# Head jobs as block products: eight of twelve instead of four of twelve, with sums formed in place

## The chip, the cores and the metric

The kernel runs on one core of one Trainium2 chip. A core has five engines that work side by side, each in its own order, and wait for one another through semaphores: TensorE (PE) does the matrix products (its loads of the stationary operand are listed apart, as PEld), VectorE (DVE), ScalarE (ACT) and GpSimd (POOL) do elementwise work, SyncE (SP) issues most of the transfers. The metric is the time of one execution of the whole program on the device, in microseconds (us); lower is better.

## What is computed

The reference is one layer of a hybrid decoder step in float32, for a prompt of 1024 tokens and 32 sample tokens (8 sequences of 4), with a width of 1024:

```python
h, gate = adaln_in(x, c, w_ada, b_ada, g_norm)         # RMS norm with scale and shift from c
(mq, mk, mv, mi, mf, mo, mz, aq, ak, av, az, gm, ga) = split_in(h @ w_in)
y_m, C, n, m = mlstm_branch(mq, mk, mv, mi, mf, mo, mz, ...)   # 4 heads, chunks of 128
q = partial_rope(aq, pos); k = partial_rope(ak, pos)
o = attn_prompt(q, k, v, sinks)                        # window of 128, 8 heads on 2 kv heads
y_a = o * silu(az)
u = sigmoid(gm) * (y_m @ w_mo) + sigmoid(ga) * (y_a @ w_ao)
x = x + gate * (u @ w_o)                               # then a final RMS norm
```

The sample tokens go through the same layer with a state (`state_C`, `state_n`, `state_m`) and a key and value cache of their own. Each operand of a large product is split into a high and a low half of reduced width; a product is the sum of three: high by high, high by low, low by high.

## The kernel before, in words

Tokens lie along the free dimension: 1024 prompt tokens and 32 sample tokens are 1056 columns, the channels lie on the 128 partitions in 8 tiles (k-tiles). The first stage normalises the input in 16 half tiles of 512 columns (`xT[token half][k]`), splits each into `h_hi` and `h_lo` (`y{p}_{k}` names the normalised tile) and also stores it to DRAM (`hD`). Every projection of h is then a *job* of 128 output channels.

A **plain job** (`job`, `piece`, L507 and L553) works through all 1056 columns in pieces of 384, 384 and 288: for each piece 8 k-tiles times three products, 72 matmuls. The jobs run in this order: `ak` and `av` with the first stage; the four query jobs `aq`; then of the twelve head jobs (`mq`, `mk`, `mv` for each of 4 heads) the first eight.

A **pair** (`Pair`, `block_products`, L1333 and L1483) takes two jobs together as a 2 x 2 block product, after the scheme of Winograd: two jobs by two halves of the contraction, times two contraction halves by two token halves, with seven products in place of eight. One product is 4 k-tiles times three, at 512 columns: 84 matmuls for a pair. It needs sums of weight blocks (formed per pair on VectorE) and the sums `t1` to `t4` of blocks of h, formed once by `sum_blocks` (L1292), which loads h from `hD` into tiles `hb`. The sample columns of a pair are 16 small products `smp` and a product `smpo` that adds them up. The products run in the order 1, 5, 6, 2, 7, 3, 4; `bx`, `bz`, `bw` and `by` are their accumulators, and `filled` copies one accumulator into the next as a start value. The 16 pairs before are: two `head_in` pairs (the last four head jobs), eight gate pairs (`ga` with `gm`), two query gate pairs (`az`), four head gate pairs (`mo` with `mz`). After them come the output products of attention (`ax` to `az`, from block sums that `att_sums` forms of the gated attention rows) and of the mLSTM branch (`g_w_mo`), then the last product (`fo`).

Between these main products stands the **side work**: 16 attention units (`unit`), four heads of the mLSTM prompt (`head`), the sample heads (`sample_head`), the conditioning of the gate (`ada_gate`), the output weights (`out_weights`), the block sums. Each is a generator. PE's order is the program's order (`mm` at L258, `tr` at L263), and a planner, `Side` (L112), decides while the program is written: it keeps a clock of estimated PE time, and after each k-tile `tick` lets due generators take a step. The streams "m" (heads and their gap), "a" (attention units: at most five at once), "x", "s" (sample heads, one at a time) and "g" each have their limits. `side.until` (L157) moves that clock forward and takes steps with no main product between them until a condition holds. The hook of the pairs (near L1966) uses it: product 6 of the last head gate pair is not written before all sample heads are done, since that pair's `samples` uses their results.

A sample head (L1152) ends with these steps: `st` (a PE product that sums its numerators), a copy to `sns` and its squared length on ScalarE, a dozen and a half small VectorE instructions (`fsden`, `fsv`, `fsr_y`, `fsr_w`), the scaling of `sns`, and the PE transpose `sty`. VectorE's, ScalarE's and POOL's order after the first stage is set by the framework's scheduler, as the instructions' operands come due; their instructions all carry L219. SP issues the transfers (L246) in its order, and some are issued on ACT's or POOL's queue.

Of the kernel before, what the change touches and what calls it, by code (L numbers as in the profile page):

```python
# [172 lines left out]
def body(tc, a):  # L173
    nc = tc.nc
    with ExitStack() as ctx:
        cp = ctx.enter_context(tc.tile_pool(name="cp", bufs=1))
        sp = ctx.enter_context(tc.tile_pool(name="sp", bufs=1))
# [13 lines left out]
            return ps.tile(shape, F32, tag="o", bufs=2, name=name)  # L191

        def ht(shape, name, dt=F32):
            return sp.tile(shape, dt, tag="half", bufs=43, name=name)

        def sm(shape, name, bufs=3, dt=F32):
            return sp.tile(shape, dt, tag=name, bufs=bufs, name=name)
# [43 lines left out]
        def dma(out, in_, late=False):  # L241
            stores(in_.tensor)
            issue(out, in_, late)

        def issue(out, in_, late=False, eng=None):
            ins = (eng or nc.sync).dma_start(out, in_)  # L246
            ins = getattr(ins, "ins", ins)
            if late:
                no_sync(ins, free)
                free.clear()  # L250
            free.append(ins)

        side = Side(stores, {"m": (2, 35.0), "a": (5,8.0), "x": (2, 0.0), "s": (1, 0.0), "g": (1, 0.0)}, 1.5)
# [47 lines left out]
        xT = [[], [], None]  # L301
# [183 lines left out]
        def raw_tile(name):  # L485
            return granule(name, "wr", 9)
# [61 lines left out]
        order = []  # L548
# [254 lines left out]
            dma(a["k_s"][124:128].rearrange("t b e -> b t e"), kns)  # L803
            dma(a["v_s"][124:128].rearrange("t b e -> b t e"), vns)

        heads_done, samples_done, units_done, products_done = [], [], [], []
        oD = [dp.tile([128, SEQ], F32, name=f"oD{g}") for g in range(4)]
        osm = cp.tile([128, NH, NS], F32, name="osm")
        yaD = [dp.tile([128, T], F32, name=f"yaD{g}") for g in range(4)]
# [176 lines left out]
        def head_jobs(h):  # L986
            q, k, v = mD[h]

            def keep(dst, smp, scale, eng):
                def ev(p, acc, c0, n):  # L990
                    t = ht([128, 384], f"mk{h}")[:, :n]
                    if eng == "v":
                        V.tensor_copy(t, acc[:, :n])
                    else:
                        S.activation(t, acc[:, :n], AF.Copy, scale=scale)
                    m = n if p < 2 else 256
                    issue(dst[:, c0:c0 + m], t[:, :m], eng=nc.scalar)
                    if p == 2:
                        G.tensor_copy(smp[:, h], t[:, 256:288])
                return ev  # L1000

            for n, dst, smp, scale in (("mq", q, qs, float(128 ** -0.5)), ("mk", k, ks, 1.0), ("mv", v, vs, 1.0)):
                if (n, h) not in order:
                    return
                i = order.index((n, h)) - order.index(None)
                if i == -4:
                    side.add("x", sum_blocks())
                if i == -1:
                    side.finish("g")
                    sc_bank[:] = po, "o+"  # L1010
                    next(work)
                job((n, h), keep(dst, smp, scale, "s"), (lambda: next(work)) if i == -1 else None)
                head_part(h, 2)
# [3 lines left out]
        def head_part(h, n):  # L1017
            parts_done[h] += n
            if parts_done[h] == 6:
                side.add("m", head(h))  # L1020
# [252 lines left out]
        blocks, formed = {}, []  # L1273
        def block(kh, th):
            return [tuple(x(4 * kh + k, 512 * th, 512) for x in (h_hi, h_lo)) for k in range(4)]

        def block_load(names, k):
            ts = []
            for kh, th in names:
                ts.append(ht([128, 512], f"hb{kh}{th}_{k}"))  # L1280
                dma(ts[-1], hD[:, 4 * kh + k, HALF[th]])
            return ts
# [6 lines left out]
        def block_tiles(n, k):  # L1289
            blocks[n].append(tuple(ht([128, 512], f"{n}{x}{k}", F32R) for x in "hl"))  # L1290

        def sum_blocks():  # L1292
            names = "t3", "t2", "t4"
            for n in names:
                blocks[n] = []
            load = lambda k: block_load(((0, 0), (0, 1), (1, 0), (1, 1)), k)
            nxt = load(0)
            yield 7.0, ""
            for k in range(4):
                b11, b12, b21, b22 = nxt  # L1300
                for n in names:
                    block_tiles(n, k)
                V.tensor_tensor(b22, b22, b12, op=ALU.subtract)
                yield 2.5, ""
                V.tensor_tensor(b11, b11, b22, op=ALU.add)
                V.tensor_tensor(b21, b21, b11, op=ALU.subtract)
                yield 5.0, ""
                if k < 3:
                    nxt = load(k + 1)
                for n, t in zip(names, (b22, b11, b21)):  # L1310
                    block_split(n, k, t)
                    yield 2.5, ""
            formed.append("t2")
            load = lambda k: block_load(((0, 0), (0, 1)), k)
            ts = [load(0), load(1)]
            yield 3.0, ""
            for b11, b12 in ts:
                V.tensor_tensor(b12, b12, b11, op=ALU.subtract)
            while not products_done:
                yield 0.5, ""  # L1320
            for k in range(4):
                b11, b12 = ts[k]
                if k > 1:
                    V.tensor_tensor(b12, b12, b11, op=ALU.subtract)
                block_split("t1", k, b12)
                if k < 2:
                    ts.append(load(k + 2))
                yield 1.5, ""
            formed.append("t1")
# [3 lines left out]
        class Pair:  # L1333
# [6 lines left out]
            def load(self):  # L1340
                for c, n in enumerate(self.names):
                    for kh in range(2):
                        t = self.raw[c, kh] = raw_tile(f"wr_{n[0]}{n[1]}_{kh}")
                        dma(t, a["w1"][JOBS[n]][:, 4 * kh:4 * kh + 4])
# [210 lines left out]

        order += [("ak", 0), ("av", 0)] + [("aq", g) for g in range(4)]
        inner = [(n, h) for h in range(NH) for n in ("mq", "mk", "mv")]
        paired = list(zip(inner[8::2], inner[9::2]))
        order += inner[:8]
        order += [None] + [("w_mo", d) for d in range(KT)]  # L1560


# [333 lines left out]
        def ada_gate():  # L1896
            s9 = cst[:, C_S9:C_S9 + 9]
            for j in range(2):
                cj = slice(j * 512, (j + 1) * 512)
                raws = []  # L1900
                for k in range(KT):
                    raws.append(ht([128, 512], f"adar_ga{j}{k}"))
                    dma(raws[-1], a["w_ada"][4 + j, :, k])
                    yield 2.0, ""
                gb = ht([128, 512], f"gb{j}")[:9]
                dma(gb, a["b_gate"][:, cj].to_broadcast((9, 512)))
                yield 5.0, "b"
                mS = ht([128, 512], f"adas_ga{j}")
                yield from ada_rows(raws, f"ga{j}", mS)
                yield 1.5, "b"  # L1910
                gp = pb([128, 512], f"gp{j}")[:9]
                mm(gp, s9, mS, start=True, stop=True)
                V.tensor_tensor(gb, gp, gb, op=ALU.add)
                V.tensor_scalar(gb, gb, 0.25, None, op0=ALU.mult)
                dma(gbD[:, cj], gb[0:1])
                for t in range(NT):
                    dma(gsD.rearrange("(b t) e -> b t e", t=NT)[:, t, cj], gb[1:9])
                yield 3.0, "b" if j == 0 else ""
            dma(c32, hD[:, :, SEQ:T])
# [46 lines left out]
        def hook(n, i):  # L1966
            if n == 0 and i in (6, 5):
                side.until(lambda: {6: "t2", 5: "t1"}[i] in formed)
            if i == 6:
                if pairs[n].kind is query_gate:  # L1970
                    side.until(lambda: len(units_done) == 16)
                side.until(lambda: len(samples_done) >= {head_in: 0, gate: 0, query_gate: 1, head_gate: pairs[n].i + 2}[pairs[n].kind])
            if (n, i) == (OUT_WEIGHTS, 6):
                side.add("g", out_weights())
# [2 lines left out]
            if n == len(pairs) - 1:  # L1977
                next(att, None)

        OUT_WEIGHTS = 4  # L1980
        LOADS = [(len(pairs) - 2, 7), (len(pairs) - 1, 5)]
        work = block_products(pairs, hook)
        att = att_products()
        for g in range(4):
            queries(g)
        side.add("g", ada_gate())
        side.add("s", sample_attention(), "b")
        blocks["t1"] = block(0, 1)
        for h in range(NH):
            head_jobs(h)  # L1990

# [62 lines left out]
        for d in range(KT):  # L2054
# [3 lines left out]
            for j in range(min(22, d * 26 // KT), min(22, (d + 1) * 26 // KT)):  # L2058
                n, k = parts[j]
# [104 lines left out]
        for i, r in enumerate(blocks_of_rows):  # L2164
            nxt = blocks_of_rows[i + 1] if i < 3 else None
# [64 lines left out]
            else:  # L2230
# [9 lines left out]
                for f, (y, (c0, n)) in enumerate(zip(Y, parts)):  # L2240
# [3 lines left out]
                    if f:  # L2244
                        V.tensor_tensor(xb[1][:, hi], xb[1][:, hi], gf[:, hi], op=ALU.mult)
                        half = norm_sum(ss[:, 2:4], 1, 2)
# [51 lines left out]


def build(d):  # L2300
    nc = bacc.Bacc("TRN2", target_bir_lowering=False, num_devices=1)
    aps = {}
    for k, v in d.items():
        aps[k] = nc.dram_tensor(k, v.shape, mybir.dt.from_np(v.dtype), kind="ExternalInput").ap()
    for k, s in OUTS.items():
        aps[k] = nc.dram_tensor(k, s, F32, kind="ExternalOutput").ap()
    with tile.TileContext(nc) as tc:
        body(tc, aps)
    return nc
# [19 lines left out]
```

## Time and profile before

| | before |
|---|---|
| median of three runs | 845.72 us (845.09 to 845.74) |
| span of the profiled execution (first to last instruction) | 843.1 us |
| PE busy | 823.9 us, 5185 instructions |
| DVE, ACT, POOL busy | 599.2, 416.0, 63.3 us |
| granted TensorE clock, mean of the span | 0.997 |
| first product of the first pair (`bx`) | 279.4 us |
| last `st` and last `sty` of a sample head | 621.1 and 634.2 us |

The three runs are times of the whole execution; of the profiled one the page gives the span alone, 2.6 us below the median of the runs. In a row of the time line stand the start in us, the duration, the engine, the line, the operation, the tile written and the tiles read with their shapes, the count of merged instructions, and, in brackets, how long the engine stood idle before and who released it. Matmuls overlap in PE, so a row's duration (0.39 for 512 columns) is longer than the distance to the next start.

### The profile page before, as it was taken

The numbers are of one execution on the slowest core, as the hardware profiler recorded it, in microseconds if no ns is written. First come the engines' busy times: TensorE is split into PE (matmuls) and PEld (weight loads), VectorE is DVE, ScalarE is ACT, GpSimd is POOL, SyncE is SP. The second block draws the span as 40 slices with busy tenths as digits, with TensorE's granted clock in tenths as the row PEclk, the third lists the DMA queues.
The fourth block names the chain that finished last, engine by engine and source line by source line (L and its number), as shares of the span: only waits on it lengthen the run. The fifth ranks groups of instructions, "written<-read, shape, count | busy, mean of one in ns | idle before, by whom it ended". The sixth has DMA issues, their size and how long they took to land.

```text
span 843.1 us, 15367 instructions
## 1 busy us (share of the span) xinstructions
PE 823.9 (98%) x5185; PEld 680.6 (81%) x5185; DVE 599.2 (71%) x1601; ACT 416.0 (49%) x1027; POOL 63.3 (8%) x108
## 2 busy tenths in 40 slices
PE   6999999999999999999999999999999999999996
PEld 3779999879989878888878777777777779997775
DVE  4887884556667586655766875788878998865676
ACT  5663346655655454554543534444436554334343
POOL 0120000000110000000000000000002104250000
PEclk9999999999999999999999999999999999999998
DMA  9996548337745653454656584556446586634522
GB/s 332 371 358 200 146 150 297 119 111 237 247 133 177 193 163 103 162 175 153 206 185 207 194 253 127 178 151 152 127 126 211 190 266 212 215 95 168 200 106 107
DMA packets 117859, 158.18 MB, mean 188 GB/s; under 512 B 29056, under 2 KB 64512, under 8 KB 117748
## 3 DMA queue, kind: packets, MB, share of 16 engines
q1 hardware_dynamic: 111556, 146.44, 55.1%
q10 hardware_dynamic: 4752, 6.56, 2.1%
q0 software_dynamic: 1472, 4.20, 1.3%
q8 instruction: 41, 0.67, 0.3%
q14 instruction: 38, 0.31, 0.1%
HBM read 113.41 MB, written 44.75 MB: 188 GB/s over the span
## 4 chain that ended last, share of the span: by engine, by line
PE 93%; DVE 4%; DMA 1%; issue 1%; ACT 1%; SPq 0%; DVEq 0%; ACTq 0%
PE by L258 10%; PE bx L258 10%; PE bw L258 10%; PE g_aq L258 6%; PE g_w_mo L258 6%; PE bz L258 5%; PE g_mk L258 4%; PE g_mq L258 4%; PE g_mv L258 3%; PE foW L258 3%; PE foX L258 3%; PE foY L258 2%; PE sc L258 2%; PE oT L258 2%; PE foZ L258 2%; PE smp L258 2%
## 5 line engine op out<-in xcount | busy, mean ns | idle before, releaser
L219 ACT ACTIVATE p<-p,nmx 128x256 f32<-128x256 f32 (+1 forms) x64 | 31.0, 486 | 26.6 <-DVE nmx L219 22.3
L258 PE MATMUL g_aq<-h_h,wh_aq 128*128 128x384 f32 (+1 forms) x96 | 32.4, 337 | 0.0
L258 PE MATMUL g_w_mo<-ym_l,wh_w_mo 128*128 128x384 f32 (+1 forms) x96 | 31.1, 324 | 0.0
L258 PE MATMUL g_aq<-h_l,wh_aq 128*128 128x384 f32 (+1 forms) x96 | 31.0, 323 | 0.0
L258 PE MATMUL g_w_mo<-ym_l,wl_w_mo 128*128 128x384 f32 (+1 forms) x96 | 31.0, 323 | 0.0
L258 PE MATMUL g_aq<-h_h,wl_aq 128*128 128x384 f32 (+1 forms) x96 | 31.0, 323 | 0.0
L258 PE MATMUL g_w_mo<-ym_h,wh_w_mo 128*128 128x384 f32 (+1 forms) x96 | 31.0, 323 | 0.0
L219 DVE CUSTOM_DVE_ANT_0 p<-sc,cst,sink 128x256 f32<-128x256 f32 (+1 forms) x64 | 26.1, 463 | 3.6 <-PE sc L258 3.5
L258 PE MATMUL g_mk<-h_h,wh_mk 128*128 128x384 f32 (+1 forms) x72 | 24.8, 344 | 0.0
L258 PE MATMUL g_mq<-h_h,wh_mq 128*128 128x384 f32 (+1 forms) x72 | 24.4, 339 | 0.0
L219 DVE TENSOR_TENSOR et<-et,cst 128x384 f32<-128x384 f32 (+1 forms) x12 | 6.2, 513 | 24.9 <-DMA et<-nmd 24.9
L219 ACT ACTIVATE gt<-gt 128x512 f32<-128x512 f32 (+1 forms) x17 | 10.4, 613 | 26.9 <-DVE gt L219 26.2
L258 PE MATMUL g_mk<-h_l,wh_mk 128*128 128x384 f32 (+1 forms) x72 | 23.3, 323 | 0.0
L258 PE MATMUL g_mq<-h_l,wh_mq 128*128 128x384 f32 (+1 forms) x72 | 23.3, 323 | 0.0
L258 PE MATMUL g_mk<-h_h,wl_mk 128*128 128x384 f32 (+1 forms) x72 | 23.2, 323 | 0.0
L258 PE MATMUL g_mq<-h_h,wl_mq 128*128 128x384 f32 (+1 forms) x72 | 23.2, 323 | 0.0
L219 ACT ACTIVATE et<-et,an 128x128 f32<-128x128 f32 x32 | 11.2, 394 | 23.1 <-DVE et L219 17.8
L258 PEld LDWEIGHTS g_aq<-h_h,wh_aq 128*128 128x128 f32 x96 | 18.0, 188 | 1.4 <-issue 1.2
L246 POOL DMA_DIRECT2D oD<-uqv x16 | 8.8, 553 | 134.1 <-ACT uqv L219 130.8
L219 ACT ACTIVATE p<-p,den 128x256 f32<-128x256 f32 (+1 forms) x32 | 14.7, 490 | 8.1 <-DVE den L219 7.9
L258 PEld LDWEIGHTS g_w_mo<-ym_h,wh_w_mo 128*128 128x128 f32 x96 | 18.0, 188 | 0.0
L258 PEld LDWEIGHTS g_w_mo<-ym_l,wh_w_mo 128*128 128x128 f32 x96 | 18.0, 188 | 0.0
(1969 smaller groups left out, 2851.8 us busy)
## 6 DMA issues: line engine op xcount, KB each, us to landing
hb<-hD SPq DMA_DIRECT2D x24, 256.0 KB
x<-xT SPq DMA_DIRECT2D x16, 256.0 KB
early_h<-w_ada SPq DMA_DIRECT2D x8, 512.0 KB
adar_ga<-w_ada SPq DMA_DIRECT2D x16, 256.0 KB
wr_ga<-w SPq DMA_DIRECT2D x16, 256.0 KB
wr_gm<-w SPq DMA_DIRECT2D x16, 256.0 KB
taD<-gt SPq DMA_DIRECT2D x16, 256.0 KB
tmD<-gt SPq DMA_DIRECT2D x16, 256.0 KB
```

What stands on the lines that cost most here:

```text
L219: ins = f(*args, **kw)
L246: ins = (eng or nc.sync).dma_start(out, in_)
L258: in_order(nc.tensor.matmul(out, lhsT, rhs, start=start, stop=stop, skip_group_check=more))
```

## The change

Four edits belong together, and four follow from them.

- The pairs take eight of the twelve head jobs: `inner[4:]` instead of `inner[8:]`. Plain are only `mq0`, `mk0`, `mv0` and `mq1`. There are 18 pairs instead of 16, four of them `head_in` pairs.
- `sum_blocks` no longer loads h from `hD` for `t2`, `t3` and `t4`. It forms the sums in the normalised tiles `xT` of the first stage, in place, and so those tiles are held until then. It is added to the planner ahead of the query jobs instead of three jobs before the first pair. Only after the plain jobs end does it load the blocks for `t1`.
- The pool of half tiles has 50 buffers instead of 43.
- From the last plain job on, stream "a" admits three attention units at once, not five.
- `ada_gate` is added ahead of the query jobs as well, not after them.
- The steps of `sum_blocks` ask for other distances (4.0 for 5.0, and 3.0 for 2.5 units of the planner's clock).
- `OUT_WEIGHTS` counts pairs: 6 for 4, which is the same gate pair as before.
- The program reserves 1024 bytes for the descriptors of software DMAs instead of the default.

```diff
         def ht(shape, name, dt=F32):
-            return sp.tile(shape, dt, tag="half", bufs=43, name=name)
+            return sp.tile(shape, dt, tag="half", bufs=50, name=name)
...
-        heads_done, samples_done, units_done, products_done = [], [], [], []
+        heads_done, samples_done, units_done, products_done, plain_ends = [], [], [], [], []
...
                 i = order.index((n, h)) - order.index(None)
-                if i == -4:
-                    side.add("x", sum_blocks())
                 if i == -1:
+                    plain_ends.append(True)
                     side.finish("g")
                     sc_bank[:] = po, "o+"
+                    side.streams["a"]["max"] = 3
                     next(work)
...
-            load = lambda k: block_load(((0, 0), (0, 1), (1, 0), (1, 1)), k)
-            nxt = load(0)
-            yield 7.0, ""
             for k in range(4):
-                b11, b12, b21, b22 = nxt
+                b11, b12, b21, b22 = (xT[th][4 * kh + k] for kh in range(2) for th in range(2))
                 for n in names:
                     block_tiles(n, k)
                 V.tensor_tensor(b22, b22, b12, op=ALU.subtract)
                 yield 2.5, ""
                 V.tensor_tensor(b11, b11, b22, op=ALU.add)
                 V.tensor_tensor(b21, b21, b11, op=ALU.subtract)
-                yield 5.0, ""
-                if k < 3:
-                    nxt = load(k + 1)
+                yield 4.0, ""
                 for n, t in zip(names, (b22, b11, b21)):
                     block_split(n, k, t)
-                    yield 2.5, ""
+                    yield 3.0, ""
             formed.append("t2")
+            while not plain_ends:
+                yield 0.5, ""
             load = lambda k: block_load(((0, 0), (0, 1)), k)
...
-        paired = list(zip(inner[8::2], inner[9::2]))
-        order += inner[:8]
+        paired = list(zip(inner[4::2], inner[5::2]))
+        order += inner[:4]
...
-        OUT_WEIGHTS = 4
+        OUT_WEIGHTS = 6
...
+        side.add("g", ada_gate())
+        side.add("x", sum_blocks())
+        blocks["t1"] = block(0, 1)
         for g in range(4):
             queries(g)
-        side.add("g", ada_gate())
         side.add("s", sample_attention(), "b")
-        blocks["t1"] = block(0, 1)
...
-    nc = bacc.Bacc("TRN2", target_bir_lowering=False, num_devices=1)
+    nc = bacc.Bacc("TRN2", target_bir_lowering=False, num_devices=1, dynamic_dma_scratch_size=1024)
```

## The prediction

> **What bounds the kernel now.** I read the page first (busy shares, chain), then the waits of TensorE, then stretches of the span, then single instructions where the change touches them.
>
> ```profile
> span 843.1 us, 15367 instructions
> PE 823.9 (98%) x5185; PEld 680.6 (81%) x5185; DVE 599.2 (71%) x1601; ACT 416.0 (49%) x1027; POOL 63.3 (8%) x108
> ...
> PE 93%; DVE 4%; DMA 1%; issue 1%; ACT 1%; SPq 0%; DVEq 0%; ACTq 0%
> ```
>
> PE is busy for 98% of the span and makes 93% of the chain that ended last. So a PE instruction more or less counts in full, and other work counts only where PE has to wait for it. PE's largest waits (total, times, longest):
>
> ```profile
> PE xc L258 <- ACT xsq L219: 6.5, 1, 6.5
> PE bx L258 <- ACT gt L219: 1.2, 1, 1.2
> PE smp L258 <- ACT hv L219: 1.0, 1, 1.0
> PE by L258 <- DVE mkv L219: 0.9, 1, 0.9
> ```
>
> The 6.5 us is the start of the program. Those of `smp` and `by`, and a smaller one of `n`, fall into the two head pairs, as the rows of part 1 show. The median of the runs, 845.72, is 2.6 us above the profiled span of 843.1. I work in differences and add them to the median.
>
> **1. Four plain jobs become two pairs (PE).** In PE's time line the spacing of the starts is what a matmul costs when the next one is ready.
>
> ```profile
> 271.01 0.34 PE L258 MATMUL g_mk<-h_l,wh_mk 128*128 128x384 f32 x1
> ...
> 273.82 0.33 PE L258 MATMUL g_mk<-h_h,wl_mk 128*128 128x384 f32 x1
> 275.74 0.30 PE L258 MATMUL g_mk<-h_h,wh_mk 128*128 128x288 f32 x1
> ...
> 277.99 0.29 PE L258 MATMUL g_mk<-h_h,wl_mk 128*128 128x288 f32 x1
> ...
> 290.87 0.71 PE L258 MATMUL n<-hv,et 128*128 128x129 f32 x4 [0.46 <-DVE C L219]
> ...
> 297.29 0.30 PE L258 MATMUL smp<-wr_mk,c 128*32 128x128 f32 x2 [0.96 <-ACT hv L219]
> ...
> 298.30 0.50 PE L258 MATMUL bx<-h_h,wh_phead_in__3732 128*128 128x512 f32 x1
> ...
> 308.67 0.50 PE L258 MATMUL by<-t4h,wh_phead_in__3898 128*128 128x512 f32 x1 [0.88 <-DVE mkv L219]
> ...
> 311.89 0.39 PE L258 MATMUL bz<-h_h,wh_phead_in__3944 128*128 128x512 f32 x1
> ...
> 317.19 0.39 PE L258 MATMUL bw<-t2h,wl_phead_in__3974 128*128 128x512 f32 x1
> ```
>
> From 271.01 to 273.82 stand 17 matmuls of 384 columns: 2.81/16 = 0.176 us each. From 275.74 to 277.99 stand 18 of 288: 2.25/17 = 0.132. From 311.89 to 317.19 stand 24 of 512: 5.30/23 = 0.230. The 16 `smp` products take 298.30 - 297.29 = 1.0. A plain job is 8 k-tiles x 3 products x pieces of 384, 384 and 288 columns; four of them are 192 x 0.176 + 96 x 0.132 = 46.5 us. A pair is 7 block products x 4 k-tiles x 3 = 84 matmuls of 512, 16 `smp` and one `smpo` (0.1, an estimate from the 64 columns beside the 288 above); two pairs are 168 x 0.230 + 2 x 1.1 = 40.8. That is 5.7 us less; the first matmul after other work takes more (0.50 against 0.39, at 298.30), and I take **-5.4**, all of it on PE's path.
>
> **2. Waits in the pairs.** The two pairs of before have 0.46 + 0.96 + 0.88 = 2.3 us of them. Two more cost 0 to 2.3. Two of the three belong to steps of a head, which run beside any product; the third is the pair's own (`mkv`). I take that one again: **+0.9**. In return the block sums `t2` are no longer formed just ahead of their first use in the first pair, where side work was pulled forward to get them. That can have caused at most 0.46 + 0.96 = 1.4; I take half, **-0.7**.
>
> **3. The block sums move beside the query jobs.** SP loses 16 loads of 256 KB (`hb`). DVE keeps the number of sums, but 12 sums and 12 splits now fall here (columns: PE, PEld, DVE, ACT, POOL busy, clock, DMA share, GB/s):
>
> ```profile
> 84.00:104.00 20.00, 20.00 (x130) 18.30 (x129) 16.00 (x55) 6.51 (x21) 0.00 (x0) 1.00 0.56 142
> 104.00:124.00 20.00, 20.00 (x134) 17.81 (x134) 17.33 (x72) 10.76 (x35) 0.71 (x1) 1.00 0.45 148
> 124.00:144.00 20.00, 20.00 (x154) 18.26 (x154) 10.67 (x42) 10.84 (x33) 1.40 (x3) 1.00 0.93 298
> ...
> 618.70 0.69 DVE L219 TENSOR_TENSOR wr_mo<-wr_mo,wr_mo 128x512 f32<-128x512 f32 x1
> ...
> 620.50 0.68 DVE L219 SCALAR_TENSOR_TENSOR hg<-hg,by 128x512 f32<-128x512 f32 x1
> ```
>
> The last two rows are DVE's; two more such lie between them, so a 512-wide DVE instruction takes 1.80/3 = 0.60. DVE is busy 44.0 of these 60 us and gets 24 x 0.60 = 14.4: 58.4 of 60. What waits behind them on DVE are the weight splits and the softmax steps, and PE waits for those. PE has no idle time there now. The price lies between 0 (they have slack) and 3 (in the first two windows alone 33.3 busy plus two thirds of 14.4 is 42.9, of 40). PE never waits in these windows today, which speaks for slack; I take **+0.5**.
>
> **4. Edits priced at nothing.** The gate conditioning starts earlier, so its 16 loads of 256 KB stand ahead of attention's on SP, with DMA at 0.45 to 0.93; a late load would hold an attention unit, which PE's order then meets as a wait like those of part 3. Some 22 more 512-wide DVE instructions (13 us) lie under PE's work. The smaller descriptor area touches only POOL's software DMAs; POOL is busy 8%, and a store that starts late has no early reader. The gate weights start at the same gate pair as before (its index moves with the pairs).
>
> **5. Pairs begin earlier with attention still open, three units at a time at most.** Counted over the PE instructions ahead of them at the spacings above, heads 2 and 3 begin 31 and 19 us later, and with them the four sample heads, which start when head 3 ends. The last head gate pair may not pass its product 6 before sample head 3 is done: the hook (L1972) lets side work go on without a main product until it is. So far that was no matter:
>
> ```profile
> 621.12 0.41 PE L258 MATMUL st<-sz,cst 128*32 128x129 f32 x2
> ...
> 634.15 0.24 PE L263 MATMUL sty<-cst,sns 32*128 32x32 f32 x1
> ...
> 621.56 0.26 ACT L219 COPY sns<-st 32x129 f32<-32x129 f32 x1 [1.48 <-PE st L258]
> ...
> 621.85 0.15 DVE L219 SCALAR_TENSOR_TENSOR fsden<-sns 32x1 f32<-32x1 f32 x1
> ...
> 626.43 0.33 DVE L219 TENSOR_SCALAR sns<-sns,fsden,fsr_y 32x128 f32<-32x128 f32 x1
> ```
>
> Thirteen us of other products lay between `st` and the transpose `sty` that ends the sample head. In the order of the changed program the last `sty` follows its `st` **directly**, and every later matmul stands behind it. (The other three keep 12 to 13 us.) So PE waits for the whole chain: copy on ACT, factors on DVE, scaling of `sns`. It took 626.76 - 621.12 = 5.6 us here, with three 512-wide DVE instructions between `fsden` and the scaling. In the changed order eight such and a 256-wide one stand there, from the sums for the output products (att_sums), which now are forced forward at the same point: 5 x 0.60 + 0.34 = 3.3 more, so 8.9 at least, less 0.3 of `st` itself: 8.6. Two of these also wait for POOL, which waits for ACT:
>
> ```profile
> 622.22 0.62 ACT L219 CAST wh_phead_gate__7498<-wr_mo 128x512 fp32r<-128x512 f32 x1
> ...
> 639.15 1.40 POOL L219 TENSOR_TENSOR yat3l<-yr,yat3h 128x512 fp32r<-128x512 f32 x1 [3.24 <-ACT yat3h L219]
> ...
> 653.06 1.28 POOL L219 TENSOR_TENSOR yab22l<-yr,yab22h 128x512 fp32r<-128x512 f32 x1 [9.27 <-ACT yab22h L219]
> ...
> 639.43 1.66 DVE L219 TENSOR_TENSOR wr_mo<-wr_mo,wr_mo 128x512 f32<-128x512 f32 x1
> ```
>
> By hand, from the issue of `st` at T: ahead of `fsden` DVE has six sums and splits to do that follow ACT copies of 0.6 each, queued behind the pair's own copy, to T + 4.7. ACT's copy and POOL's 1.3 for `yab22l` end at T + 6.5; three sums and a split, 0.6 each with small steps between, to T + 9; the copies `yat2h`, `yab21h` and POOL's `yab21l` to T + 11.1; a last sum, three small steps and the scaling to T + 12.7. POOL's instruction between these can stretch one on DVE from 0.69 to 1.66, as beside the one at 639.15, hence 13.5 at most. Between 8.6 and 13.5 I take **+12.0**, near the hand count.
>
> After such a gap the clock may be lower. The trace has a gap at either end:
>
> ```profile
> 5.00:10.00 5.00, 3.51 (x25) 1.76 (x26) 2.69 (x7) 2.35 (x5) 0.00 (x0) 1.00 0.99 343
> ...
> 835.00:840.00 5.00, 1.12 (x10) 0.92 (x8) 3.65 (x13) 1.44 (x4) 0.00 (x0) 0.85 0.27 105
> 840.00:843.10 3.10, 0.00 (x0) 0.00 (x0) 0.00 (x0) 0.00 (x0) 0.00 (x0) 0.50 0.44 169
> ...
> 7.37 5.25 PE L258 MATMUL xs<-xsq,one 128*32 128x512 f32 x15
> ...
> 14.64 3.25 PE L258 MATMUL xs<-xsq,one 128*32 128x512 f32 x16
> ```
>
> PE ends at 836.1; the granted clock then is 0.85 and 0.50, so it falls within some us of idling. After the idle 6.5 us at the start it reads 1.00, yet 16 products go at 0.35 us instead of 0.20, a loss of 2.4 if the clock was the cause. Between 0 and 2.4 I take a third, since the column reads 1.00: **+0.8**. The Trainium skill, TensorE: Matmul & The Clock Gate, "HAM oscillation", holds that an idle gap above about 3.4 us puts the array back to half its clock, and that some 3.4 us of work are needed to lift it again. By that rule the gap here costs an estimated 1.7 us instead, and the sum would be 854.7. The trace agrees on the fall (0.50 at the end), and shows no return.
>
> **The sum.** 845.7 - 5.4 + 0.9 - 0.7 + 0.5 = 841.0 without the new wait; + 12.0 + 0.8 = **853.8**.
>
> **Rivals.** (a) Faster: the forced wait is short, since what stands ahead of `sns` on DVE is done before `st` issues. At 2.5 us the time is 843.5; it is faster by 0.2% as long as the wait is below 3.0. For it: side work was pulled forward in before as well, and cost at most 1.4. Against: eight 512-wide instructions stand behind `fsden`, which reads `st`'s result; DVE works in order. (b) No change: the wait is the 5.6 us of before less 0.3: 846.3. Same objection. (c) Slower still: DVE's crowding of part 3 costs its full 3, and the pairs their 2.3: 853.8 + 2.5 + 1.4 = 857.7. For it: 58.4 of 60 us; against: PE waits nowhere there today.
>
> **How the numbers follow.** Forecast 0.68, (a) 0.12, (b) 0.08, (c) 0.12. About 0.2% (1.7 us) is what a measurement of this kernel can tell from no change: faster means below 844.0, slower above 847.4. So faster 0.12, same 0.08, slower 0.80. The range goes from 846, which holds (b) and the lower end of the wait (841.0 + 8.6 = 849.6), to 858 for (c).
>
> **What would show it.** In the profile after: PE 5.4 us less busy, near 818.5; a wait of `sty` for DVE `sns` of 9 to 13 us, about 550 to 620 us into the span, as PE's largest; a granted clock below 1.00 in that stretch; no wait of PE for weight splits between 64 and 145 us; DVE above 0.9 there; waits of `by` for `mkv` near 1.8 in total. The prediction is wrong if that wait is under 3 us, or if PE is not less busy.

## The result

The changed kernel takes 860.3 us (median of four runs, 859.13 to 860.53) against 845.4 for the one before (844.71 to 845.74): 1.0181 times as long, 95% interval 1.0168 to 1.0195. The forecast was 853.8 us in a range of 846 to 858. It is slower, as forecast, by 14.9 us in place of 8.1, and outside the range.

The page of the profiled execution (859.13 us, span 857.4) begins:

```profile
span 857.4 us, 15202 instructions
...
PE 820.6 (96%) x5133; PEld 669.3 (78%) x5133; DVE 612.0 (71%) x1623; ACT 421.8 (49%) x1034; POOL 62.5 (7%) x104
```

The span grew by 14.3 us. PE is busy 3.3 us less than the 823.9 of before, and idle 36.8 us where it was idle 19.2. So the new pairs saved PE work, and 17.6 us of new idle time buried the saving. The waits of PE say where (total, times, longest):

```profile
PE sty L263 <- DVE sns L219: 15.9, 1, 15.9
PE xc L258 <- ACT xsq L219: 6.3, 1, 6.3
PE S L258 <- DVE C L219: 2.3, 2, 1.3
PE sU L258 <- DVE Cs L219: 1.9, 1, 1.9
PE bw L258 <- ACT bw L219: 1.0, 1, 1.0
```

One wait of 15.9 us, at the place in PE's order that part 5 of the prediction names, though at 641 to 657 us into the span and not at 550 to 620. The three waits of the two old pairs (`smp` for `hv`, `by` for `mkv`, `n` for `C`) are gone. PE's time line around the wait, and the stretches with the granted clock (PE, PEld, DVE, ACT, POOL busy, clock, DMA share, GB/s):

```profile
640.86 0.41 PE L258 MATMUL st<-sz,cst 128*32 128x129 f32 x2
657.19 0.28 PE L263 MATMUL sty<-cst,sns 32*128 32x32 f32 x1 [15.92 <-DVE sns L219]
657.40 0.80 PE L258 MATMUL bw<-t2h,wh_phead_gate__7498 128*128 128x512 f32 x1
...
658.42 0.63 PE L258 MATMUL bw<-t2h,wl_phead_gate__7499 128*128 128x512 f32 x1
...
661.40 0.56 PE L258 MATMUL bw<-t2h,wh_phead_gate__7498 128*128 128x512 f32 x1
661.80 0.39 PE L258 MATMUL bw<-t2l,wh_phead_gate__7498 128*128 128x512 f32 x1
```

```profile
641.00:644.50 3.50, 0.27 (x2) 0.00 (x0) 3.50 (x7) 2.94 (x8) 0.00 (x0) 1.00 0.90 294
644.50:657.00 12.50, 0.00 (x0) 0.00 (x0) 11.20 (x29) 4.75 (x8) 4.67 (x3) 0.51 0.60 150
657.00:661.50 4.50, 4.31 (x11) 3.41 (x12) 0.80 (x3) 0.00 (x0) 0.00 (x0) 0.50 0.72 204
```

`sty` stands right behind `st`, and the next product behind `sty`. The ten products from 657.40 to 661.80 take 0.44 us each instead of 0.23, because the clock is at 0.50: 2.1 us lost beside the wait. In the wait PE stands still while DVE is busy 11.2 of 12.5 us. The chain there, from DVE's and POOL's time lines:

```profile
646.44 0.14 DVE L219 SCALAR_TENSOR_TENSOR fsden<-sns 32x1 f32<-32x1 f32 x1
...
647.11 0.67 DVE L219 TENSOR_TENSOR yat4l<-yr,yat4h 128x512 fp32r<-128x512 f32 x1
...
649.34 0.69 DVE L219 TENSOR_TENSOR yr<-yr 128x512 f32<-128x512 f32 x1 [1.08 <-POOL yab22l L219]
...
650.80 1.78 DVE L219 TENSOR_TENSOR yr<-yr 128x512 f32<-128x512 f32 x1
...
654.04 1.11 DVE L219 SCALAR_TENSOR_TENSOR fsr_w<-fsr_y,fsv 32x1 f32<-32x1 f32 x1
...
656.71 0.34 DVE L219 TENSOR_SCALAR sns<-sns,fsden,fsr_y 32x128 f32<-32x128 f32 x1
```

```profile
647.16 2.15 POOL L219 TENSOR_TENSOR yab22l<-yr,yab22h 128x512 fp32r<-128x512 f32 x1 [11.61 <-ACT yab22h L219]
650.77 1.26 POOL L219 TENSOR_TENSOR yat3l<-yr,yat3h 128x512 fp32r<-128x512 f32 x1 [1.46 <-ACT yat3h L219]
653.88 1.26 POOL L219 TENSOR_TENSOR yab21l<-yr,yab21h 128x512 fp32r<-128x512 f32 x1 [1.85 <-issue]
```

From T = 640.86 on, `fsden` starts at T + 5.6 (hand count 4.7), `yab22l` ends at T + 8.5 (6.5), `yab21l` at T + 14.3 (11.1), and `sns` is ready at T + 16.2 (12.7). Two DVE instructions, 1.78 for 0.69 and 1.11 for 0.21, are stretched while POOL works beside them. Beside POOL's first instruction it was the other way round: DVE's `yat4l` kept its 0.67, and POOL took 2.15 where its next two took 1.26.

### The profile page after: what moved, and what is told of

Read it like the earlier page. It is cut to its first block, busy times and chain, and to the rows that moved or that the text cites. A ratio compares the mean times of both kernels' runs of the same rounds, so it can differ in the third digit from the quotient of the medians.

```text
span 857.4 us, 15202 instructions
## 1 busy us (share of the span) xinstructions
PE 820.6 (96%) x5133; PEld 669.3 (78%) x5133; DVE 612.0 (71%) x1623; ACT 421.8 (49%) x1034; POOL 62.5 (7%) x104
## 5 line engine op out<-in xcount | busy, mean ns | idle before, releaser
L219 ACT ACTIVATE et<-et,an 128x128 f32<-128x128 f32 x32 | 11.5, 394 | 19.3 <-DVE et L219 19.2
L258 PE MATMUL sc<-ukv,uqv 64*128 64x256 f32 (+1 forms) x128 | 18.4, 390 | 0.4 <-DVE p L219 0.4
L258 PEld LDWEIGHTS g_aq<-h_l,wh_aq 128*128 128x128 f32 x96 | 18.1, 188 | 0.0
L258 PEld LDWEIGHTS g_aq<-h_h,wl_aq 128*128 128x128 f32 x96 | 18.0, 188 | 0.0
L258 PEld LDWEIGHTS g_w_mo<-ym_l,wl_w_mo 128*128 128x128 f32 x96 | 18.0, 188 | 0.0
L219 DVE COPY p<-pt 128x512 f32<-128x512 f32 (+1 forms) x16 | 10.4, 652 | 9.6 <-PE pt L263 9.6
L219 ACT ACTIVATE sq<-rows_h 128x512 f32<-128x512 f32 (+2 forms) x14 | 8.2, 582 | 17.7 <-issue 12.0
L219 DVE SCALAR_TENSOR_TENSOR tgw_mo<-tgw_mo,g_w_mo 128x384 f32<-128x384 f32 (+1 forms) x24 | 12.2, 515 | 6.4 <-PE g_w_mo L258 6.4
L258 PE MATMUL g_mq<-h_h,wh_mq 128*128 128x384 f32 (+1 forms) x48 | 16.5, 344 | 0.0
L263 PE MATMUL sty<-cst,sns 32*128 32x32 f32 x4 | 1.0, 252 | 15.9 <-DVE sns L219 15.9
```

What stands on the lines that cost most here:

```text
L219: ins = f(*args, **kw)
L258: in_order(nc.tensor.matmul(out, lhsT, rhs, start=start, stop=stop, skip_group_check=more))
L263: in_order(nc.tensor.transpose(out, in_, idn))
```

## The experiments

The theory: the late sample head puts `sty` right behind `st`, and this wait with its half clock is the loss. The rivals: PE is held up by VectorE in the last pairs whatever stands in PE's order; the clock has nothing to do with the slow products; the moved sums cost time of their own. All comparisons are with the kernel before on the same chip (844.8 to 845.1 there).

**The wait later.** The last pair waits before product 4, not product 6:

```diff
-            if i == 6:
-                if pairs[n].kind is query_gate:
-                    side.until(lambda: len(units_done) == 16)
+            if i == 6 and pairs[n].kind is query_gate:
+                side.until(lambda: len(units_done) == 16)
+            if i == (4 if n == len(pairs) - 1 else 6):
                 side.until(lambda: len(samples_done) >= {...}[pairs[n].kind])
...
                     Y = filled(pa, "by", W, n)
-                    job_.samples_end()
+                    if nxt:
+                        job_.samples_end()
...
+                if i == 4 and not nxt:
+                    job_.samples_end()
```

> The changed kernel, but the last head gate pair waits for sample head 3 before its product 4 instead of before its product 6, and adds up its sample columns after product 4. In PE's order some 9.5 us of products then stand between the last st and its sty (an estimate from the instructions between them at 0.23 us for 512 columns). Theory (the 15.9 us wait of sty and the slow clock behind it are the loss): the wait falls to 0 to 4 us and, if below about 2.4 us, the 2.0 us of half clock go as well; 842.5 to 848 us. Rival (the work behind the wait is late in any case, because VectorE is the bound there): another wait of 10 us or more takes its place within the next 20 us, 856 to 860 us.

It took 850.43 us (six runs, 846.86 to 852.6), 1.0060 times before (1.0042 to 1.0079). In its profile (span 845.1, of the run with 846.86) the wait of `sty` is 2.13 us. So most of the loss goes with the wait's place, and nothing of 10 us takes its place. The half clock, expected to go with a wait below some 2.4 us, stayed behind this one (last section). The median is above the 842.5 to 848 expected. What separates the other five runs from the profiled one was not traced; their mean granted clock was 0.990 to 0.994 against its 0.996, which points to more time at half clock. The other waits of the changed kernel are still there: `S` for `C` 2.6, `sU` for `Cs` 1.9, `n` 1.2.

**The sums out of the chain.** The second `att_sums` is added before product 2 in place of product 5, that is behind product 6 and two products later (not one, as the expectation says); the wait stays:

```diff
-        LOADS = [(len(pairs) - 2, 7), (len(pairs) - 1, 5)]
+        LOADS = [(len(pairs) - 2, 7), (len(pairs) - 1, 2)]
```

> The changed kernel, but the second set of sums for the attention output products (att_sums 1) is added to the planner one product later in the last pair, after product 6, so that it is not forced forward between st and sty; the wait stays where it is. Theory (VectorE and POOL work of att_sums inside the chain from st to sns makes up the half of the wait): about 4 VectorE instructions of 512 columns remain between fsden and the scaling instead of 8, the wait is 8 to 10 us instead of 15.9, time 852 to 855 us. Rival (the sums are late for the output products anyway, so what leaves the chain comes back as a wait of aw or ax): 858 to 861 us.

862.48 us (860.73 to 864.27), 1.0205 times before (1.0183 to 1.0226). The theory was right on the wait and wrong on the time, which lies above the rival's range too. In PE's time line:

```profile
418.89 0.71 PE L258 MATMUL S<-hq,hk 128*128 128x128 f32 x4 [2.06 <-DVE C L219]
...
655.59 0.28 PE L263 MATMUL sty<-cst,sns 32*128 32x32 f32 x1 [8.19 <-DVE sns L219]
...
678.09 0.50 PE L258 MATMUL az<-ym_h,wh_ao0A 128*128 128x512 f32 x1 [2.96 <-DVE ym_h L219]
```

The wait of `sty` is 8.2 us, so the sums made up half of it. But they were then late for the output products (`az` for `ym_h`, 3.0), and PE was busy 5.6 us longer (826.2) than in the first profile of the changed kernel, with the same instructions: the clock fell three times, at 420, 645 and 680 us. The rival named such a return. So half the wait is DVE work that is needed soon in any case.

**PE kept busy in the wait.** 56 products without use, behind the last `st`:

```diff
             mm(tot[:NS], cst[:, C_S32:C_S32 + NS], ns4, start=True, stop=True)
+            if h == NH - 1:
+                fill, (b, _) = po([128, 512], "fill"), blocks["b11"][0]
+                for _ in range(56):
+                    in_order(nc.tensor.matmul(fill, b[:, 0:128], b, start=True, stop=True))
```

> The changed kernel with 56 added products of 128 by 512 (operands that lie ready, result not used) directly behind the last st: 13.0 us of PE work inside the wait, nothing else moved. Theory (the half clock comes from the idle time): idle falls to about 3 us, the products behind sty run at 0.23 us from the first on, 2.0 us less: 858 to 858.7 us. Rival (those products are slow for another reason, the release or transfers beside them): 860 to 860.6 us.

866.19 us (863.66 to 867.19), 1.0244 times before (1.0224 to 1.0264); both expectations on the time failed. The products are there in full, and behind them PE no longer waits for `sty`:

```profile
643.66 12.98 PE L1223 MATMUL fill<-h_h 128*128 128x512 f32 x56
656.57 0.24 PE L263 MATMUL sty<-cst,sns 32*128 32x32 f32 x1
656.75 0.50 PE L258 MATMUL bw<-t2h,wh_phead_gate__7498 128*128 128x512 f32 x1
657.08 0.40 PE L258 MATMUL bw<-t2l,wh_phead_gate__7498 128*128 128x512 f32 x1
...
659.17 0.39 PE L258 MATMUL bw<-t2l,wh_phead_gate__7498 128*128 128x512 f32 x1
```

The same products behind `sty` go at 0.23 us from the first on (657.08 to 659.17 are nine steps of 0.232). So the half clock does come from the idle time. The total went up all the same. The filler also changed the order of the other engines: the sums, which stood inside the chain, now ran only behind the filler (DVE stood idle for 6.7 us until 656.68, released by `fill`), DVE came to `hg1z` only at 673.3, and `by` waited 4.9 us for it, with a half clock of its own. This run shows the clock term, but not its price in the whole, and with the sums out of the chain it does not show how long `sty` itself would have waited.

**The sums in place alone.** The pairing of before, with all the other edits:

```diff
-        paired = list(zip(inner[4::2], inner[5::2]))
-        order += inner[:4]
+        paired = list(zip(inner[8::2], inner[9::2]))
+        order += inner[:8]
...
-        OUT_WEIGHTS = 6
+        OUT_WEIGHTS = 4
```

> The changed kernel with the pairing of before: eight plain head jobs and two head pairs, the out weights at pair 4 again; block sums in place and early, the earlier gate conditioning, 50 half tiles, and at most three attention units during pairs all stay. In PE's order 12 us of products stand between the last st and sty, as before. Theory (moving the sums costs nothing, and what the pairs' start cost is gained): 844 to 846 us, no wait of sty. Rival (VectorE's crowding beside the query jobs costs PE up to 3 us): 847 to 849 us, with new waits of g_aq, g_mq or sc between 64 and 145 us.

850.85 us (848.79 to 851.25), 1.0061 times before (1.0042 to 1.0080): slower, but not where the rival put it. PE does not wait between 64 and 145 us. It waits at 426 us. From DVE's, ACT's and PE's time lines:

```profile
424.74 0.43 DVE L219 TENSOR_TENSOR et<-et,cst 128x256 f32<-128x256 f32 x1 [4.75 <-DMA et<-nmd]
...
425.56 0.46 ACT L219 ACTIVATE yt<-ty,vec 128x256 f32<-128x256 f32 x1
...
426.07 0.90 PE L263 MATMUL ty<-cst,et 128*128 128x128 f32 x3 [4.28 <-ACT yt L219]
```

A load of head 3 (`et`) lands late, ACT has work on it ahead of `yt`, and `ty` waits for `yt`. In the kernel before DVE waited for the same load, 5.9 us, while PE had its operands. Whether the load is late because of the loads of the output weights beside it was tried next:

```diff
-        OUT_WEIGHTS = 4
+        OUT_WEIGHTS = 6
```

> The kernel with the sums in place alone (eight plain jobs, 850.9 us), output weights begun at pair 6 instead of 4. Theory (its wait of ty for yt, 4.3 us at 426 us, comes from the last load of head 3 landing behind the loads of the output weights): the wait goes, 845 to 847 us. Rival (the wait comes from ScalarE's order alone): it stays, 849 to 851 us.

845.61 us (844.45 to 849.71), 1.0010 times before (0.9995 to 1.0024). The wait of `ty` is 0.4 us, and the loss against the kernel before falls from 5.8 us to 0.8, so the output weights' place made some 5 us. The load did not take much longer beside them, though (5.4 us from its issue to DVE's work on it, against 4.7): SP issued it later, at 419.29 against 414.83, while PE stood only 1.4 us behind. SP had first to store `gt`, which DVE formed at 415.26 against 410.93. What made DVE late with `gt` was not traced further. In-place sums beside the query jobs cost nothing that can be measured.

**The changed kernel again, and heads earlier.** Four kernels on one chip:

> The changed kernel itself, beside the next three on one chip: 859 to 861 us, its wait of sty 15 to 16.5 us, ten products at half clock behind it.

863.24 us (860.46 to 865.7), 1.0208 times before (1.0181 to 1.0235), above the 859 to 861 expected; the wait of `sty` 15.2 us. In this profile `S` for `C` waits 2.9 us at 419.5 and is followed by half clock to 425. This time is also the nearest measure for the runs with the late wait, the later sums and the filler, which were on the same chip: against it they took 12.8 us less, 0.8 less and 3.0 more.

```diff
-        side = Side(stores, {"m": (2, 35.0), "a": (5,8.0), ...
+        side = Side(stores, {"m": (2, 25.0), "a": (5,8.0), ...
```

> The changed kernel with heads admitted 25 instead of 35 units of the planner's clock apart; nothing else. Head 3 and the sample heads move some 10 and 6 us forward in PE's order, and 6.3 us of products (estimate from their count) stand between the last st and sty. Theory (the loss is the distance from st to sty that the late heads took away): the wait of sty is 4 to 10 us, 849 to 854 us. Rival (the heads' place is of no matter; VectorE is the bound in the last pair): the wait or another one behind it stays above 12 us in all, 857 to 861 us.

847.39 us (846.0 to 849.88), 1.0033 times before (1.0020 to 1.0046). In PE's time line:

```profile
632.63 0.41 PE L258 MATMUL st<-sz,cst 128*32 128x129 f32 x2
...
645.04 0.28 PE L263 MATMUL sty<-cst,sns 32*128 32x32 f32 x1 [5.59 <-DVE sns L219]
```

Moving heads by one number takes 15.9 us off the time: the wait falls from 15.2 to 5.6 us, and `sU` for `Cs` and `S` for `C` at 415 us no longer appear. This is more than the theory expected (849 to 854), as it priced only `sty`. The rival falls: where the heads stand decides. The same edit in the kernel before leaves its program exactly as it was, so the kernel before could not have gained by it.

With four units as well (`["max"] = 4`):

> The changed kernel with four instead of three attention units during pairs and heads 25 apart. The sample heads move some 11 us forward, and 10.4 us of products stand between the last st and sty (before: 12 to 13). Theory: the wait of sty is 0 to 5 us, without or with a short drop of the clock, 843 to 849 us, and the wait of sU for Cs (1.9) goes too, since the sums of att_sums no longer stand ahead of it. Rival: as above, 857 to 861 us.

848.05 us (846.53 to 849.82), 1.0039 times before (1.0027 to 1.0052). `sty` does not wait at all, but the time is not below the run before it. Three other waits of 1.8 to 3.3 us (`pt` for `mx` at 236, `S` for `C` at 411, `by` for `hg1z` at 661) are each followed by some 3.4 us with the clock at 0.50. With the late wait added to this one:

> The kernel of the run before this one, and the last pair waits for sample head 3 before product 4 instead of product 6: 12.5 us of products between the last st and sty. Theory: no wait of sty above 1 us and no half clock behind it; PE's saving of 5.4 us shows, less the 2 to 4 us of other small waits of the changed kernel (S for C, n, bw): 841 to 845 us, at or below the kernel before. Rival: waits of the head steps come back in other places, 847 to 852 us, as in the run with the late wait alone.

845.21 us (842.79 to 848.38), 1.0005 times before (0.9990 to 1.0021): the loss of the changed kernel is gone, but also the saving, to a wait of `S` for `C` of 3.1 us and the half clock behind it.

**Versions with both.** The late wait and heads 25 apart, three units:

> The changed kernel (three attention units during pairs) with heads 25 apart and the last pair's wait before product 4: 12.6 us of products stand between the last st and sty. Theory: from the profile with heads 25 apart alone (span 844.8), its wait of sty (5.6) and the half clock behind it (1.9) go: span near 837.5, time 839 to 842 us, 0.3 to 0.7% below the kernel before, the saving of the two new pairs. Rival (other head waits return once sty does not hold PE back, as with four units): 844 to 847 us.

841.23 us (839.98 to 842.37), 0.9954 times before (0.9938 to 0.9969). Its page and the end of its sample head in PE's time line:

```profile
span 840.1 us, 15210 instructions
...
PE 819.7 (98%) x5133; PEld 667.3 (79%) x5133; DVE 607.9 (72%) x1623; ACT 420.4 (50%) x1034; POOL 63.3 (8%) x104
```

```profile
633.88 0.41 PE L258 MATMUL st<-sz,cst 128*32 128x129 f32 x2
...
646.84 0.24 PE L263 MATMUL sty<-cst,sns 32*128 32x32 f32 x1
```

Thirteen us of products cover the chain again, there is no wait of `sty` and no fall of the clock before the end. PE is busy 4.2 us less than in the kernel before and idle 1.2 us more. This version beats both kernels. With the output weights two pairs later:

> The run before this one with the output weights begun two gate pairs later (8 instead of 6), so that their loads do not stand beside the last loads of head 3. Theory (the run-to-run wait of S for C near 410 us comes from loads that land late behind these weights): no such wait in the profile, and 0 to 3 us less than the run before. Rival (the wait has another cause, or the weights are late for the last product): the same or 1 to 5 us more.

844.81 us (843.71 to 846.35), 0.9996 times before (0.9984 to 1.0008). Its wait at 410 us was not there in the first place, and another comes in at a query gate (`bx` for `zt` 2.0), while that of `by` for `gt` (1.5 before, 1.6 now) moves to a later gate: the rival. In the version with four units, where that wait was there:

> The kernel with four units, heads 25 apart and the late wait (845.2 us), with the output weights begun at pair 8 instead of 6. Theory: its wait of S for C (3.1 us at 410 us, with 1.7 us of half clock behind it) goes: 840 to 842 us. Rival: the wait stays, 844 to 846 us.

841.57 us (840.0 to 843.05), 0.9960 times before (0.9947 to 0.9972). `S` for `C` is down from 3.1 to 0.3 us and the half clock is gone, as the theory said.

## Why the prediction was right and wrong

*Part 1 was right, and near in size.* PE is busy 3.3 us less; without the 2.1 us that the half clock adds to ten products this is 5.4, as taken. The version with heads 25 apart and the late wait, whose clock stays up until the end, shows 4.2, which is the cleaner measure.

*Part 2 was wrong in its parts.* The waits of `by` for `mkv` did not double, they disappeared, as did the other two of the old pairs. Others came: `S` for `C` at 294 and 415 us, `bw` for `bw`, `by` for `ztz`. All waits of PE but `sty` come to 13.9 us against 12.1: +1.8, where parts 2 and 3 had +0.7.

*Part 3 was right that there is slack.* The sums now stand from 71 to 148 us. DVE is nearly full in the first of these stretches (19.7 of 20 us, where it was 14.7), but in the 60 us from 84 on it is busy 47.2, not the 58.4 forecast, and PE does not wait:

```profile
64.00:84.00 20.00, 19.99 (x140) 19.50 (x131) 19.68 (x63) 8.18 (x18) 0.19 (x1) 1.00 0.71 227
84.00:104.00 20.00, 20.00 (x130) 16.29 (x129) 16.96 (x60) 8.22 (x24) 0.00 (x0) 1.00 0.75 191
```

The slack covered it all; the kernel with the sums in place confirms it, at 845.61 us. Rival (c) named crowding as the way to a time near 858, and did not happen.

*Part 4 missed one thing.* "The gate weights start at the same gate pair as before" was priced at nothing. It is the output weights that the index starts, and their loads meet the last loads of head 3. In the kernel with the sums alone this cost some 5 us; in the changed kernel the wait of `S` for `C` near 410 to 420 us, 1.3 and 2.9 us in its two profiles, stands at the same loads. That the same cause makes it there was shown only for the version with four units.

*Part 5 is the step that failed, by its size.* The mechanism and the place in PE's order were right: `sty` directly behind `st`, the chain over ACT, DVE and POOL, and the sums of `att_sums` forced into it. The wait was taken as 12.0 with 13.5 as its end; it measured 15.9 and 15.2. The hand count was short at each joint: DVE's work ahead of `fsden` by 0.9 us, POOL's first instruction by 2.0 (it took 2.15, not 1.28, and began 1.1 later, behind its ACT copy), and the DVE instructions that ran beside POOL were stretched twice, not once. The chance for the other signs, 0.2, rested on a short wait, and both rivals (a) and (b) fell on the argument made against them: DVE works in order.

*The clock* was taken at +0.8, a third of a bound of 2.4 (which counted 16 products where the row has 15; with 15 it is 2.2). It cost 2.1. The rule that the Trainium skill gives in TensorE: Matmul & The Clock Gate, "HAM oscillation", would have given an estimated 1.7 and 854.7 in all, nearer than my third of the bound. The trace agrees with its half clock, which here lasted 4.5 us after work resumed (0.50 from 657.2 to about 661.7), longer than the prediction's 3.4. On the gap that it takes, above some 3.4 us by that rule, the runs differ: waits of 2.1 us were enough (last section), and the measurement decides.

In sum, for the span: 12.0 became 15.9 (+3.9), 0.8 became 2.1 (+1.3), 0.7 became 1.8 (+1.1), and PE's saving held. From the 8.1 us forecast that leads to 14.4, against 14.3 measured. The median lies 0.6 us further off than the spans show.

## What to carry to other kernels

When a wait is written into the program's order, look at how much work the planner still has to put between the producer and the consumer. Here a saving of 4 to 5 us shifted the heads, used up 13 us of cover and cost 15.9. Price such a chain with every instruction that the in-order engines hold between its ends, and allow for stretching where VectorE and GpSimd work side by side (here two instructions of VectorE and one of GpSimd). And after taking out work, tune the release of the side work again: one number for the distance of the heads gave back 15.9 us, and with the wait four products later the change became 0.46% faster than the kernel before.

## What the runs showed of the hardware

The clock falls after much shorter waits than that of `sty`. In the run with the late wait PE idled 2.1 us ahead of `sty`, and the products behind it went at half speed:

```profile
657.24 0.28 PE L263 MATMUL sty<-cst,sns 32*128 32x32 f32 x1 [2.13 <-DVE sns L219]
657.45 0.79 PE L258 MATMUL by<-t4h,wh_phead_gate__7669 128*128 128x512 f32 x1
...
659.75 0.63 PE L258 MATMUL by<-t4h,wl_phead_gate__7670 128*128 128x512 f32 x1
```

Steps of 0.43 us; the granted clock was 0.50 from 657.2 to 660.6, so the 2.1 us wait cost some 1.6 us more. The same happened at every longer wait of PE after the start of the program, in all these runs, and behind one of 2.06 us (sums later). Below that the length does not decide. The same wait of `sU`, 1.9 us, was followed by a half clock in two runs, the later sums and the changed kernel again:

```profile
646.17 0.39 PE L258 MATMUL sU<-vm,skn 96*128 96x258 f32 x1 [1.88 <-DVE Cs L219]
...
647.34 0.63 PE L258 MATMUL bz<-h_l,wh_phead_gate__7470 128*128 128x512 f32 x1
647.77 0.63 PE L258 MATMUL bz<-h_h,wl_phead_gate__7471 128*128 128x512 f32 x1
```

These rows are of the changed kernel again; the clock fell near 647.3, before the long wait of `sty` began. In three other runs, the first profile of the changed kernel among them, the same wait was followed by none. Nor was one of 2.01 us, in the run with the output weights two pairs later, while one of 1.78 us in the version with four units was:

```profile
539.75 0.50 PE L258 MATMUL bx<-h_h,wh_pquery_gate__6368 128*128 128x512 f32 x1 [2.01 <-DVE zt L219]
540.09 0.40 PE L258 MATMUL bx<-h_l,wh_pquery_gate__6368 128*128 128x512 f32 x1
540.33 0.40 PE L258 MATMUL bx<-h_h,wl_pquery_gate__6369 128*128 128x512 f32 x1
```

So in these runs a wait of PE from 2.06 us on brought the half clock each time and cost some 1.5 us or more beyond its own length; one between 1.8 and 2.0 us did so only sometimes, and one up to 1.6 us never. What decides in between was not found. The version with four units paid this three times.
